# Low weight parts by accumulating DMA, the compression steps moved, and the last block of the last projection in halves

## The chip, the core and the metric

The kernel runs on one core of one Trainium2 chip. The core has TensorE (PE in the profile; its weight loads are shown as PEld), VectorE (DVE), ScalarE (ACT), GpSimd (POOL) and SyncE (SP), which issues the DMAs of this kernel. All engines run at the same time and wait for one another through semaphores. The metric is the device time of one execution in microseconds (us), as the median of several runs.

## What is computed

The reference is a small decoder trunk over 256 tokens of width 1024: one layer with a gated short convolution, one with a sparse attention, and around each mixer two half-step feed-forwards (d_ff = 2816). Between the two layers the keys and values are made once, among them a compressed set (blocks of 32 tokens through a small two-layer network). Cut to what the change touches:

```python
def swiglu_ffn(x, w_in, w_out):
    gate, up = jnp.split(x @ w_in, 2, axis=-1)
    return (jax.nn.silu(gate) * up) @ w_out

def compress(raw, pe, w1, w2):
    ...
    return jax.nn.gelu(blk @ w1) @ w2

def reference(x, ...):
    h = x
    for i in range(DEPTH):
        if i == N_A_LAYERS:
            kv = shared_kv(h, ...)
        h = h + 0.5 * swiglu_ffn(rmsnorm(h, ffn1_norm[i]), ffn1_w_in[i], ffn1_w_out[i])
        hn = rmsnorm(h, mix_norm[i])
        if i < N_A_LAYERS:
            h = h + short_conv_mixer(hn, conv_w_in[i], conv_w[i], conv_w_out[i])
        else:
            h = h + nsa_mixer(hn, attn_w_q[j], attn_q_norm[j], attn_w_o[j], rel_bias, kv)
        h = h + 0.5 * swiglu_ffn(rmsnorm(h, ffn2_norm[i]), ffn2_w_in[i], ffn2_w_out[i])
    return h
```

All inputs and the output are float32.

## The kernel before, in words

**Split products.** Every large product is made of three: each operand is split into a high part, rounded to the type fp32r, and a low part, the rest. The product is high x high, low x high and high x low. With the activations as the moving operand (512 columns: 256 tokens of the high part and 256 of the low part side by side) a weight tile of 128 x 128 takes two matmuls: its high part against all 512 columns and its low part against the 256 columns of the high part. Method half (L430) issues them; a_pass runs all high ones of a group and then all low ones, or the other way round, and each call begins with the kind with which the call before ended (turn).

**The weight stream.** Class Stream brings the weights in. A chunk of 2048 columns (1 MB) is loaded by SP into one of three staging buffers (tile ws, L197). A chunk holds two units of 1024 columns; a unit is 8 weight tiles. Method high casts a unit on ScalarE into a tile wh (L238). Method low subtracts on VectorE: wl = ws - wh (L266). Six buffers exist for each of wh and wl, used in turn, so a unit takes the buffers of the unit six places before, and its cast and its subtraction wait until PE has done with those. A staging buffer is free for the next load when both of its units have been read. Method pump emits high and low of the next units wherever PE's program has given buffers back (done). Units are numbered in the order of use: 0 to 43 are the first feed-forward's in projection (two a step, 22 steps), 44 to 65 its out projection, 66 to 89 the convolution's in projection (three a step).

**In and out projections.** ffn_in runs 22 steps f of two units (gate and up), 16 matmuls of each width; the evacuation of a step (ffn_evac, called through weave, which pumps the stream between its parts) runs on ScalarE and VectorE under the next step. out_proj makes 8 blocks c of the output; each takes 22 weight tiles in a row of the stream, that is 2.75 units. After each block out_evac adds it to h and prepares the next stage's operand: ScalarE and VectorE split it into xs, GpSimd sums its squares.

**Background of the second layer's first feed-forward.** Function bg(f) is called after step f of that ffn_in and holds what makes the shared keys and values: k_trans (transposes of the keys through PE), rh_split (split of the raw blocks), c_hidden (16 matmuls of 256 columns with the two units of a compression weight, W1AT tells after which step), c_total (its halves added by a small product, then gelu on GpSimd), c_second, kc_norm, kc_trans and c_values. The compression weights stand in the stream behind the units of step W1AT[0] and W1AT[1].

**The last out projection.** out_pairs makes the last projection into the output from 11 pairs p of inner blocks. For a pair not in PLAIN it uses seven products of sums in place of eight (a scheme in the manner of Strassen and Winograd); for a pair in PLAIN the eight plain ones. A product is three matmuls of 512 columns (L1415), here with the activations as the stationary operand. The sums of weights and of activations for the first kind are made on VectorE (sums, L167, and Pairs.add). Each pair's weights are prepared one or two pairs ahead (prepare, with pair_high, L161, and pair_low, L172). The eight products collect in eight banks m[1] to m[8]; m[1], m[6], m[7] and m[5] are shared by several output blocks, m[2], m[3], m[4] and m[8] belong to one each. After the last seven-product pair (last) the shared sums go through ScalarE, VectorE and GpSimd into p11, p12, p21 and p22, while PE does the remaining plain pairs; then each block gets its own bank added (L1432) and is stored (L1444).

Nothing plans this order at run time: each engine's program is as the code emits it, and each works it off in that order.

Of the kernel before, what the change touches and what calls it, by code (L numbers as in the profile page):

```python
# [9 lines left out]
F32 = mybir.dt.float32  # L10
# [3 lines left out]
ALU = mybir.AluOpType  # L14
# [48 lines left out]
def trunk(ctx, tc, A, out):  # L63
# [45 lines left out]
    class Stream:  # L109
# [133 lines left out]
        def low(self):  # L243

            if not self.half:
                return
            half = self.half.pop(0)
            if len(half) == 6 and not isinstance(half, list):
                self.pair_low(*half)
                return  # L250
            if isinstance(half, list):
                for v, t in half:
                    ve.tensor_tensor(out=t[:, :, 1], in0=v, in1=t[:, :, 0].bitcast(F32), op=ALU.subtract)
                self.units.append(tuple(t for _, t in half))
                return
            src, h = half
            if isinstance(h, Halves):
                l = Halves()
                for x in range(2):
                    ve.tensor_tensor(out=l.t[x], in0=src[:, x * 512:(x + 1) * 512], in1=h.t[x].bitcast(F32), op=ALU.subtract)  # L260
                self.units.append((h, l))
                return
            l = mk([P, 1024], "wl", NBUF, F32R)
            if len(src.shape) == 3:
                l = l.rearrange("p (a n) -> p a n", n=512)
            ve.tensor_tensor(out=l, in0=src, in1=h.bitcast(F32), op=ALU.subtract)  # L266
            if len(src.shape) == 3:
                h, l = [t.rearrange("p a n -> p (a n)") for t in (h, l)]
            self.units.append((h, l))
# [19 lines left out]
                self.pump()  # L289

    W = Stream()
    W1AT = (11, 14)
    W.add(A["ffn1_w_in"][0])
    W.add(A["ffn1_w_out"][0])
    W.add(A["conv_w_in"])
# [14 lines left out]
    W.spare = set(range(len(W.where) - 2, len(W.where) + 1))  # L310
    W.add(A["ffn2_w_in"][1])
    NP = NF // 2
    PLAIN = (0, 2, 4, 6, 8, 10)
    TURNS = (3, 5, 7, 9)

    def second_home(p):
# [675 lines left out]
    def bg(f):  # L992
# [7 lines left out]
                po.tensor_tensor(out=v, in0=v, in1=r[:, tt * 8:tt * 8 + 8, None].to_broadcast([P, 8, 64]), op=ALU.mult)  # L1000
        elif f in (2, 4, 5, 8):
            c_blocks((2, 4, 5, 8).index(f))
        elif f in (6, 7):
            k_trans(f - 6)
        elif f == 9:
            kv["rk"] = rh_split(0)
        elif f == 10:
            kv["rv"] = rh_split(1)
            W.limit = NBUF
        elif f == W1AT[0]:  # L1010
            kv["ak"] = c_hidden(kv["rk"])
        elif f == 12:
            kv["ak"] = c_total(kv["ak"])
        elif f == W1AT[1]:
            kv["av"] = c_hidden(kv["rv"])
        elif f == 15:
            kv["av"] = c_total(kv["av"])
            kv["kc"] = kc_norm(c_second(kv["ak"], 0))
        elif f == 17:
            kc_trans(kv["kc"])  # L1020
        elif f == 18:
            c_values(kv["av"])

    hid = ffn_in(xs, None, R1, bg)
# [369 lines left out]
    def out_pairs(left, rows):  # L1394
# [7 lines left out]
        for p in range(NP):  # L1402
# [2 lines left out]
                todo[p] = {n: [(x, b[i]), (y, b[i + 2])] for n, i, x, y in ((2, 0, a11, a12), (3, 1, a11, a12), (4, 0, a21, a22), (8, 1, a21, a22))}  # L1405
            else:
                todo[p] = {n: [(left[p][n - 1], right[n])] for n in right}
        total = {n: sum(len(t.get(n, ())) for t in todo.values()) for n in m}

        def product(p, *which):  # L1410
            for n in which:
# [32 lines left out]
            sy.dma_start(out[tt * P:(tt + 1) * P, 512 * x + c.start * P:512 * x + c.stop * P], o[:, c].rearrange("p a m -> p (a m)"))  # L1444

        W.freed += 1 << 10
        last = max(p for p in range(NP) if p not in PLAIN)
        for p in range(last + 1):
            product(p, *(2, 4 if p else 8) if p in PLAIN else (1, 2))
            prepare(p)  # L1450
# [8 lines left out]
        u3 = add(u2, 7, u2, None)  # L1459
        p21, p22 = plus(u3, 1, hT[1, 0]), plus(u3, 1, hT[1, 1])  # L1460
        for n, tt, x, o in ((2, 0, 0, p11), (3, 0, 1, p12), (4, 1, 0, p21), (8, 1, 1, p22)):
            for p in range(last + 1, NP):
                product(p, n)
            if n == 3:
                add(p12, 5, p12, 0)
                add(p22, 5, p22, 1)
            for c in (slice(0, 2), slice(2, 4)) if n == 8 else (slice(0, 4),):
                store(tt, x, add(o, n, o, tt, c), c)

    out_pairs(hid.left, X["rows"])  # L1470

# [69 lines left out]
```

## Time and profile before

| | |
|---|---|
| median of 3 runs | 967.3 us (966.65 to 968.2) |
| profiled execution, own time | 967.22 us |
| its span, first to last instruction | 965.4 us |
| granted TensorE clock | 0.999 |
| VectorE subtractions of the stream (L266, from ws) | 263, 326.2 us in all |
| ScalarE casts of the stream (L238, from ws) | 263, 272.2 us in all |
| read from HBM | 175.52 MB, 183 GB/s over the span |

How to read the lines: a line of a group names the code line, the engine, the operation, the tile written and those read, the shapes and the count; then the busy time, the mean duration of one in ns, and the idle time of the engine just before them with what ended most of it. A line in order of time begins with the start and the time in us, and ends with the idle time before it, where there was any, and the engine that ended it. A line of stretches gives the stretch, its length, then for PE, PEld, DVE, ACT and POOL the busy time and the number of instructions, the granted clock, the DMA engines' busy share and GB/s. Matmuls overlap: one of 512 columns is listed with 0.39 us, but the next can start before its end, so the distance of starts is what it costs.

The 40 slices of the page, each 24.1 us:

```profile
PE   9999999999999999999999999999999999999998
DVE  6988776668889888767659788866588788878896
ACT  7665553355556665644548787653579656656563
POOL 1000001144470100011321021001337350000002
DMA  7665554545536974555535556454520354467362
```

### The profile page before, as it was taken

The page shows a single profiled execution, that of the slowest core. Times are in us where ns is not written, and L with a number is a line of the kernel's source. Part 1 is how long each engine was busy: PE and PEld are TensorE (multiplying, and loading weights), DVE is VectorE, ACT ScalarE, POOL GpSimd, SP SyncE. Part 2 cuts the span into 40 slices and gives each one's busy share as a digit, 9 for nine tenths or more (in the row PEclk, how much of TensorE's full clock was granted, in tenths as well). Part 3 has the DMA queues.
Part 4 walks back from the last instruction along what each step waited for, and adds up shares of the span by engine and source line. Part 5 has one row for each costly group of instructions (what it writes and reads, how often), then busy time and mean ns, then how long its engine had stood idle before and what let it go on. Part 6 is the DMA issues. An engine that isn't in the chain of part 4 may idle for free.

```text
span 965.4 us, 14668 instructions
## 1 busy us (share of the span) xinstructions
PE 958.4 (99%) x5597; PEld 839.1 (87%) x5597; DVE 754.2 (78%) x1212; ACT 582.0 (60%) x982; POOL 173.0 (18%) x266
## 2 busy tenths in 40 slices
PE   9999999999999999999999999999999999999998
PEld 7888888888888888888888888888987888888886
DVE  6988776668889888767659788866588788878896
ACT  7665553355556665644548787653579656656563
POOL 1000001144470100011321021001337350000002
PEclk9999999999999999999999999999999999999999
DMA  7665554545536974555535556454520354467362
GB/s 294 231 213 180 187 206 175 186 166 210 188 135 228 272 238 176 188 204 182 211 131 182 192 206 251 174 189 168 218 89 1 132 218 155 152 217 257 106 205 88
DMA packets 36422, 178.60 MB, mean 185 GB/s; under 512 B 3424, under 2 KB 7152, under 8 KB 18560
## 3 DMA queue, kind: packets, MB, share of 16 engines
q1 hardware_dynamic: 36352, 177.67, 52.1%
q8 instruction: 44, 0.72, 0.3%
q14 instruction: 26, 0.21, 0.1%
HBM read 175.52 MB, written 1.08 MB: 183 GB/s over the span
## 4 chain that ended last, share of the span: by engine, by line
PE 94%; DVE 2%; ACT 2%; DMA 1%; issue 0%; SPq 0%; DVEq 0%
PE mm L430 53%; PE a L430 26%; PE a L1415 4%; PE mm L1415 2%; PE mm L1181 1%; PE a L1246 1%; PE a L812 1%; PE a L814 1%; PE a L813 1%; DMA base<-in_first_dram 1%; PE a L1226 1%; PE mm L655 1%; PE a L694 1%; DVE pr L1189 0%; ACT act L914 0%; ACT pr L1200 0%
## 5 line engine op out<-in xcount | busy, mean ns | idle before, releaser
L266 DVE TENSOR_TENSOR wl<-ws,wh 128x1024 fp32r<-128x1024 f32 x263 | 326.2, 1251 | 67.6 <-ACT wh L238 41.6
L430 PE MATMUL mm<-xs,wh 128*128 128x512 f32 x1480 | 348.8, 390 | 0.0
L430 PEld LDWEIGHTS mm<-xs,wh 128*128 128x128 f32 x1480 | 273.7, 188 | 54.3 <-DVE xs L383 0.2
L238 ACT CAST wh<-ws 128x1024 fp32r<-128x1024 f32 x263 | 272.2, 1046 | 35.6 <-PE a L430 21.1
L430 PEld LDWEIGHTS mm<-xs,wl 128*128 128x128 f32 x1480 | 185.5, 192 | 4.3
L430 PE MATMUL mm<-xs,wl 128*128 128x256 f32 x1480 | 188.3, 283 | 0.0
L430 PE MATMUL a<-act,wh 128*128 128x512 f32 x608 | 141.7, 390 | 0.0
L430 PEld LDWEIGHTS a<-act,wh 128*128 128x128 f32 x608 | 113.0, 188 | 22.7
L449 DVE TENSOR_TENSOR t<-mm,t 128x512 f32<-128x512 f32 x95 | 65.2, 686 | 61.1 <-ACT t L448 60.5
L448 ACT COPY t<-mm 128x512 f32<-128x512 f32 x95 | 55.5, 584 | 75.5 <-PE mm L430 75.1
L430 PEld LDWEIGHTS a<-act,wl 128*128 128x128 f32 x608 | 75.7, 192 | 1.6
L430 PE MATMUL a<-act,wl 128*128 128x256 f32 x608 | 76.4, 283 | 0.0
L473 ACT ACTIVATE t<-t 128x256 f32<-128x256 f32 x88 | 36.8, 419 | 56.5 <-DVE t L460 56.4
L379 ACT ACTIVATE xs<-base 128x256 fp32r<-128x256 f32 x48 | 24.1, 506 | 77.5 <-DVE base L573 62.1
L460 DVE TENSOR_TENSOR t<-t,R 128x512 f32<-128x512 f32 (+1 forms) x88 | 57.1, 649 | 2.6
L442 ACT CAST act<-t 128x256 fp32r<-128x256 f32 x91 | 37.0, 407 | 28.8 <-DVE t L743 18.2
L397 POOL TENSOR_TENSOR t<-base 128x256 f32<-128x256 f32 x35 | 26.2, 750 | 134.7 <-DVE base L573 108.5
L394 POOL TENSOR_TENSOR sq<-base 128x256 f32<-128x256 f32 x5 | 3.1, 613 | 229.2 <-DVE base L573 220.8
L443 DVE TENSOR_TENSOR act<-t,act 128x256 fp32r<-128x256 f32 x91 | 39.0, 428 | 5.7 <-ACT act L442 5.7
L383 DVE SCALAR_TENSOR_TENSOR xs<-base,xs 128x256 fp32r<-128x256 f32 x48 | 29.4, 616 | 17.5 <-ACT xs L379 17.4
L474 DVE TENSOR_TENSOR t<-t,t 128x256 f32<-128x256 f32 x88 | 36.9, 419 | 4.0 <-ACT t L473 3.9
L1440 POOL TENSOR_TENSOR t<-t,base 128x512 f32<-128x512 f32 x4 | 5.1, 1292 | 166.9 <-ACT t L1438 166.9
(313 smaller groups left out, 1144.9 us busy)
## 6 DMA issues: line engine op xcount, KB each, us to landing
ws<-in_ffn_w_in_dram SPq DMA_DIRECT2D x69, 1024.0 KB, 4.8
ws<-in_ffn_w_out_dram SPq DMA_DIRECT2D x33, 1024.0 KB, 4.6
ws<-in_conv_w_in_dram SPq DMA_DIRECT2D x12, 1024.0 KB, 4.6
base<-in_ffn_w_in_dram SPq DMA_DIRECT2D x11, 1024.0 KB, 5.2
ws<-in_w_kv_dram SPq DMA_DIRECT2D x6, 1024.0 KB, 4.8
base<-in_ffn_w_pairs_dram SPq DMA_DIRECT2D x12, 512.0 KB, 4.9
kt<-in_ffn_w_in_dram SPq DMA_DIRECT2D x5, 1024.0 KB, 7.6
ws<-in_conv_w_out_dram SPq DMA_DIRECT2D x4, 1024.0 KB, 4.8
```

Of the source, the lines that this page charges most:

```text
L238: ac.copy(h, src)
L266: ve.tensor_tensor(out=l, in0=src, in1=h.bitcast(F32), op=ALU.subtract)
L383: ve.scalar_tensor_tensor(out=xs[c][:, T:], in0=h[c], scalar=gt[:, g + c:g + c + 1], in1=xs[c][:, :T].bitcast(F32), op0=ALU.mult, op1=ALU. ...
L430: pe.matmul(o if x == 0 else o[:, :T], u[x][:, q * P:(q + 1) * P], rhs if x == 0 else rhs[:, :T], start=start, stop=stop, skip_group_check ...
L442: ac.copy(dst[:, :T], src)
L443: ve.tensor_tensor(out=dst[:, T:], in0=src, in1=dst[:, :T].bitcast(F32), op=ALU.subtract)
L448: ac.copy(r, o[:, :, T:])
L449: ve.tensor_tensor(out=r, in0=o[:, :, :T], in1=r, op=ALU.add)
L460: ve.tensor_tensor(out=r, in0=r, in1=R[:, None, :].to_broadcast([P, n, T]), op=ALU.mult)
L473: ac.activation(s, r[:, 0], AF.Silu)
L474: ve.tensor_tensor(out=s, in0=s, in1=r[:, 1], op=ALU.mult)
L1415: pe.matmul(m[n], x, w, start=(count[n] == 0 and i == 0), stop=(count[n] == total[n] - 1 and i == 2), skip_group_check=True)
```

## The change

Three edits.

1. In Stream.low, the units whose number is in BYDMA = range(12, 80, 4) don't get their low part from VectorE. ScalarE writes -src into the low tile, whose type rounds it as the cast rounds the high part; then GpSimd issues a DMA that adds src to it.
2. In bg, k_trans of both halves and both c_hidden are called after step 13 (before: 6, 7, 11 and 14), both c_total after 15 (12 and 15), c_second and kc_norm after 17 (15), kc_trans and c_values after 19 (17 and 18). W1AT = (13, 13) puts both compression weights behind step 13 in the stream.
3. PLAIN has pair 9 in place of pair 8, so that the last seven-product pair is 8 and two plain pairs, 9 and 10, come after it. The last block (p22) gets its m[8] of the earlier pairs added ahead of time; its products of pairs 9 and 10 are made in two halves of 256 columns, each in a bank of its own, and each half is added and stored by itself.

```diff
@@ Stream.low
             l = mk([P, 1024], "wl", NBUF, F32R)
             if len(src.shape) == 3:
                 l = l.rearrange("p (a n) -> p a n", n=512)
-            ve.tensor_tensor(out=l, in0=src, in1=h.bitcast(F32), op=ALU.subtract)
+            if len(self.units) in BYDMA:
+                ac.activation(l, src, AF.Copy, scale=-1.0)
+                po.dma_start(l, src, accum_op=ALU.add)
+            else:
+                ve.tensor_tensor(out=l, in0=src, in1=h.bitcast(F32), op=ALU.subtract)
@@ trunk
-    W1AT = (11, 14)
+    W1AT = (13, 13)
...
-    PLAIN = (0, 2, 4, 6, 8, 10)
+    BYDMA = range(12, 80, 4)
+    PLAIN = (0, 2, 4, 6, 9, 10)
@@ bg
-        elif f in (6, 7):
-            k_trans(f - 6)
...
         elif f == W1AT[0]:
-            kv["ak"] = c_hidden(kv["rk"])
-        elif f == 12:
-            kv["ak"] = c_total(kv["ak"])
-        elif f == W1AT[1]:
-            kv["av"] = c_hidden(kv["rv"])
+            for tt in range(2):
+                k_trans(tt)
+            kv["ak"], kv["av"] = c_hidden(kv["rk"]), c_hidden(kv["rv"])
         elif f == 15:
-            kv["av"] = c_total(kv["av"])
+            kv["ak"], kv["av"] = c_total(kv["ak"]), c_total(kv["av"])
+        elif f == 17:
             kv["kc"] = kc_norm(c_second(kv["ak"], 0))
-        elif f == 17:
+        elif f == 19:
             kc_trans(kv["kc"])
-        elif f == 18:
             c_values(kv["av"])
@@ out_pairs
-        total = {n: sum(len(t.get(n, ())) for t in todo.values()) for n in m}
+        last = max(p for p in range(NP) if p not in PLAIN)
+        total = {n: sum(len(t.get(n, ())) for p, t in todo.items() if n != 8 or p <= last) for n in m}
...
         for n, tt, x, o in ((2, 0, 0, p11), (3, 0, 1, p12), (4, 1, 0, p21), (8, 1, 1, p22)):
+            if n == 8:
+                for c in (slice(0, 2), slice(2, 4)):
+                    z = bank([P, 2, P])
+                    left = [(xs, [t[:, at, c.start * P:c.stop * P] for t in W.pair[p, kind]]) for p in range(last + 1, NP) for xs, (kind, at) in todo[p][8]]
+                    for k, ((xh, xl), (wh, wl)) in enumerate(left):
+                        for i, (a, w) in enumerate(((xh, wh), (xl, wh), (xh, wl))):
+                            pe.matmul(z.rearrange("p a m -> p (a m)"), a, w, start=(k == 0 and i == 0), stop=(k == len(left) - 1 and i == 2))
+                    ve.scalar_tensor_tensor(out=p22[:, c], in0=z, scalar=rows[:, 1:2], in1=p22[:, c], op0=ALU.mult, op1=ALU.add)
+                    store(1, 1, p22, c)
+                break
             for p in range(last + 1, NP):
                 product(p, n)
-            if n == 3:
+            if n == 2:
                 add(p12, 5, p12, 0)
+            store(tt, x, add(o, n, o, tt))
+            if n == 2:
                 add(p22, 5, p22, 1)
-            for c in (slice(0, 2), slice(2, 4)) if n == 8 else (slice(0, 4),):
-                store(tt, x, add(o, n, o, tt, c), c)
+                add(p22, 8, p22, 1)
```

More of the change, by code (lines that the diff above doesn't have):

```diff
@@ L1446, in out_pairs @@
         W.freed += 1 << 10
-        last = max(p for p in range(NP) if p not in PLAIN)
         for p in range(last + 1):
```

## The prediction

> **What bounds the kernel now.** I read the page first (busy shares, then the chain that ended last), then the busy time by stretches, the waits of TensorE's weight loads between 24 and 473 us, and the instructions in order of time at the places that the change touches.
>
> ```profile
> span 965.4 us, 14668 instructions
> PE 958.4 (99%) x5597; PEld 839.1 (87%) x5597; DVE 754.2 (78%) x1212; ACT 582.0 (60%) x982; POOL 173.0 (18%) x266
> PE 94%; DVE 2%; ACT 2%; DMA 1%; issue 0%; SPq 0%; DVEq 0%
> L266 DVE TENSOR_TENSOR wl<-ws,wh 128x1024 fp32r<-128x1024 f32 x263 | 326.2, 1251 | 67.6 <-ACT wh L238 41.6
> 22.00:473.00 451.00, 451.00 (x2592) 398.98 (x2591) 353.98 (x472) 252.47 (x367) 83.09 (x107) 1.00 0.57 199
> PEld mm L430 <- DVE xs L383: 0.2, 1, 0.2
> 24.98 105.59 PE mm L430 x608
> 130.57 61.09 PE a L430 x352
> ```
>
> TensorE is busy for 99% of the span. A busy PE need not be at its peak, so the second question is whether its matmuls follow one another at a fixed pace. They do:
>
> ```profile
> 67.36 4.00 PE L430 MATMUL mm<-xs,wl 128*128 128x256 f32 x32
> 71.19 7.44 PE L430 MATMUL mm<-xs,wh 128*128 128x512 f32 x32
> 78.47 1.72 PE L430 MATMUL mm<-xs,wl 128*128 128x256 f32 x13
> ```
>
> From 67.36 to 71.19 are 32 matmuls of 256 columns, 0.120 us each; from 71.19 to 78.47 are 32 of 512 columns, 0.2275 each. The chain holds the same pace: 608 matmuls, half of each width, in 105.59 us are 0.1737 each, the mean of the two. In the 451 us from 22 to 473 PE shows no idle time and its loads waited 0.2 us. So in the stage where VectorE is relieved, nothing waits for VectorE, and every microsecond for which PE is made to wait is added to the end. Gains can come only from places where PE waits or the tail runs alone.
>
> **The change part by part.**
>
> *First feed-forward, low parts.* Units 12, 16, ... 76 (17 of them, range(12, 80, 4)) lose a VectorE subtraction of 1.22 us each. That is some 21 us of VectorE, worth nothing by the rows above. Added on each: one ScalarE copy (the cast of the same size takes 1.04), a GpSimd DMA that reads the staged unit and adds it into the low tile (512 KB), and PE's wait for its landing. The question is which units have their low part ready soon enough. In the steady part of the feed-forward:
>
> ```profile
> 64.41 1.05 ACT L238 CAST wh<-ws 128x1024 fp32r<-128x1024 f32 x1
> 65.88 1.22 DVE L266 TENSOR_TENSOR wl<-ws,wh 128x1024 fp32r<-128x1024 f32 x1
> ```
>
> This is unit 24; its low matmuls are those at 78.47 in the fence above. Low part ready at 67.10: 11.4 us of lead. With the copy at 65.5 to 66.5, a transfer may take 11.9 us before PE waits. The staging buffer is held until landing, so the load that reuses it starts some 4 us later; the casts are also about 10 us ahead of PE, which hides it. ScalarE's extra 17 us over some 190 us (it is busy 252 of 451 us) hides in its idle time.
>
> The out projection is different. Each output block uses 22 weight tiles, a unit has 8, and blocks alternate in the order of their high and low passes, so two low passes stand back to back. Unit 52 is the ninth of the projection: tiles 64 to 71, of which block 2 (tiles 44 to 65) needs two at the end of its low pass.
>
> ```profile
> 137.80 5.40 PE L430 MATMUL a<-act,wh 128*128 128x512 f32 x23
> 143.04 5.44 PE L430 MATMUL a<-act,wl 128*128 128x256 f32 x44
> 148.31 10.16 PE L430 MATMUL a<-act,wh 128*128 128x512 f32 x44
> 140.36 3.07 ACT L238 CAST wh<-ws 128x1024 fp32r<-128x1024 f32 x3
> 143.53 3.50 DVE L266 TENSOR_TENSOR wl<-ws,wh 128x1024 fp32r<-128x1024 f32 x3 [2.56 <-PE a L430]
> 139.99 0.61 POOL L394 TENSOR_TENSOR sq<-base 128x256 f32<-128x256 f32 x1 [120.10 <-DVE base L573]
> 148.06 0.61 POOL L397 TENSOR_TENSOR t<-base 128x256 f32<-128x256 f32 x1 [7.45 <-DVE base L573]
> ```
>
> The 44 low matmuls at 143.04 are blocks 1 and 2. The first two finish unit 46, whose low buffer (six of them in turn) unit 52 takes: hence VectorE's 2.56 us wait until 143.53. The 43rd, at 143.04 + 42 x 0.120 = 148.07, is the first use of unit 52. Today 143.53 + 1.22 leaves 3.3 us. In the changed kernel ScalarE waits in VectorE's place, ends its copy at about 143.53 + 1.05 = 144.6, and the transfer has 148.07 - 144.6 = 3.5 us. Behind the waiting copy on ScalarE stand the casts of units 53 and 54, not needed before 153; on GpSimd nothing stands before 148.06, so the DMA goes out at once.
>
> No row of this trace shows an accumulating DMA or one issued by GpSimd. The nearest:
>
> ```profile
> base<-t SPq DMA_DIRECT2D x16, 64.0 KB, 2.1
> out_dram<-t SPq DMA_DIRECT2D x3, 256.0 KB, 2.0
> ws<-in_ffn_w_out_dram SPq DMA_DIRECT2D x33, 1024.0 KB, 4.6
> base<-in_ffn_w_pairs_dram SPq DMA_DIRECT2D x12, 512.0 KB, 4.9
> kt<-in_ffn_w_in_dram SPq DMA_DIRECT2D x5, 1024.0 KB, 7.6
> ```
>
> Lower end 2.0 us (half the bytes, a plain store), upper end 7.6 (the slowest issue of 1024 KB). An add has to read both operands, so 512 KB of result are 1024 KB read: the row of 4.6 is the nearest, and with 0.2 for the step from ScalarE to GpSimd I take 4.8. Then unit 52 is there at 149.4, and PE waits 1.3 us (0 at the lower end, 4.1 at the upper).
>
> The Trainium skill weighs in here: "Collectives: The Full Stack", section The bandwidth ceiling: the fold count and why AG ≠ RS ≠ AR, says that the add in the DMA path costs no time itself but two source reads. "DMA: Bandwidth & Descriptors", section Anatomy of one DMA — SWDGE (gpsimd) path, gives 2.0 us plus bytes over 436 GB/s; with 1.05 MB read that is an estimate of 4.4 us, and the sum below would be 0.4 lower. The row of 4.6 agrees within 0.2; an add by DMA no run here shows yet.
>
> The second narrow place is unit 72, in the conv projection:
>
> ```profile
> 200.67 1.05 ACT L238 CAST wh<-ws 128x1024 fp32r<-128x1024 f32 x1
> 201.97 1.31 DVE L266 TENSOR_TENSOR wl<-ws,wh 128x1024 fp32r<-128x1024 f32 x1
> 201.59 0.61 POOL L754 TENSOR_TENSOR R<-R 128x256 f32<-128x256 f32 x1 [4.77 <-DVE R L412]
> 208.43 2.08 PE L430 MATMUL mm<-xs,wl 128*128 128x256 f32 x16
> ```
>
> The copy would end at 202.8, and PE starts this low pass at 208.43: 5.6 us. At 4.8 it costs nothing, at 7.6 it costs 2.0. GpSimd's conv products (L729 to L735) queue behind the DMA; they feed only the out projection much later. The nearest of the others is unit 56, eight tiles into block 4:
>
> ```profile
> 151.31 1.05 ACT L238 CAST wh<-ws 128x1024 fp32r<-128x1024 f32 x1 [0.75 <-PE a L430]
> 158.31 1.96 PE L430 MATMUL a<-act,wl 128*128 128x256 f32 x15
> ```
>
> Its copy would end at 153.4; blocks 3 and 4 run their low passes from 158.31, and its first tile is the 31st matmul, at 161.9: 8.5 us, enough at either end.
>
> *Compression moved* (k_trans, both hidden products at f = 13, both totals at 15, the rest at 17 and 19). PE's products are the same ones.
>
> ```profile
> 573.36 0.52 PEld L936 LDWEIGHTS a<-both,t 128*128 128x128 f32 x4 [0.26 <-ACT t L928]
> 601.14 3.81 PE L430 MATMUL mm<-xs,wh 128*128 128x512 f32 x16
> 605.11 3.92 PE L430 MATMUL mm<-xs,wh 128*128 128x512 f32 x16
> ```
>
> At f = 12 the total's product waits 0.26 us for ScalarE's copy, made one step earlier; two steps later it will not. After the small products the next 16 matmuls take 3.92 instead of 3.81; such returns fall from six (f = 6, 7, 12, 15, 17, 18) to four. I take -0.26 - 2 x 0.1 = about -0.4, bounds -0.7 and +0.5 (the four hidden-layer units are now eaten in a row, 3.9 us of PE for 5 us of VectorE, covered by the pair of matmul groups on either side).
>
> *Last projection.* Pair 8 takes the seven-product form and pair 9 the plain one: as many products as before. Pairs 7 and 8 are now neighbours, and VectorE's sums and splits bunch:
>
> ```profile
> 938.12 2.36 DVE L172 TENSOR_TENSOR wl<-kt,wh 128x1024 fp32r<-128x1024 f32 x2 [0.47 <-ACT wh L161]
> 940.40 3.49 DVE L172 TENSOR_TENSOR wl<-base,wh 128x1024 fp32r<-128x1024 f32 x3
> 944.41 2.67 DVE L167 TENSOR_TENSOR base<-base 128x1024 f32<-128x1024 f32 x3
> 944.78 0.62 PE L1415 MATMUL a<-wh,act 128*128 128x512 f32 x2
> ```
>
> Two low parts of pair 8 (1.2 + 0.7) slip in ahead of 938.12, so pair 7's end at 941.2; sums (2.67) to 943.9; casts and low parts of pair 8's other kinds to 946.3 and 947.4. PE starts pair 8 at 945.46 (944.78 plus three matmuls) and after two products, 6 x 0.227 = 1.36, wants the first at 946.8: a lead of 0.5 to 1 us. No wait; if a cast slips by 2 us, +1.
>
> The end:
>
> ```profile
> 960.95 0.39 PE L1415 MATMUL mm<-wl,act 128*128 128x512 f32 x1
> 961.38 0.88 DVE L1432 SCALAR_TENSOR_TENSOR t<-mm,sm,t 128x256 f32<-128x256 f32 x2 [0.47 <-PE mm L1415]
> ```
>
> Today both half evacuations (0.44 each) follow the last matmul. In the changed kernel the first half's runs under the second half's twelve matmuls (1.44 us), so one goes: -0.44. For it PE does 24 matmuls of 256 columns instead of 12 of 512: 24 x 0.120 - 12 x 0.227 = +0.16. Net -0.3 (bounds -0.7, the whole pair and its store; +0.4, if VectorE's added sums delay the first half). With 48 closing matmuls instead of 24, the sums of the four blocks have more cover than now.
>
> Sum: 0 for VectorE, +1.3 unit 52, 0 unit 72, -0.4 compression, -0.3 tail = +0.6. The profiled execution took 967.2 (span 965.4 and 1.8 around it), the median of the runs shown is 967.3: the forecast is 967.9.
>
> **Rivals.**
>
> 1. *The transfer is slow: PE waits instead of VectorE* (slower). At 7.6 us unit 52 costs 4.1, unit 72 2.0; less 0.7 that is +5.4: 972.7. For it: the 7.6 row, DMA engines 57% busy in this stretch. Against: unit 52's transfer meets few loads, since their staging buffers are just being freed. It decides from about 6.0 us per transfer, where the sum passes +1.9.
> 2. *The transfer is quick, 3.5 us or less*: no wait at all, only compression and tail remain, -0.7: 966.6. For it: 2.0 and 2.1 us for smaller copies. Against: twice the bytes of the largest of these.
> 3. *VectorE does slow PE in a way that no wait shows* (faster). If a tenth of the 21 us came back, 964.5. Against it: the even pace of 0.120 and 0.2275.
> 4. *The change doesn't do what it says*: the tail saves nothing because the first half's evacuation stands behind the other blocks' on VectorE; +0.4 instead of -0.3, so 968.6. It lies inside the forecast's own range.
>
> **How the numbers follow.** Forecast with rival 4 (transfer of 3.8 to 6 us): 0.42. Rival 2: 0.25. Rival 1: 0.26. Rival 3: 0.07. About 0.2% (1.9 us) is what a measurement of this kernel can tell from no change. Faster by more: 0.07 (rival 3). Within: the forecast and rival 2, 0.67. Slower: 0.26. The range leaves out most of rival 3 and the part of rival 1 beyond its worked price: 966.2 (rival 2 with the tail's better bound) to 972.7.
>
> **What would show it.** A PE wait for a DMA near 148 and none near 78: unit 52. Low tiles landing within 3.5 us of their copy: rival 2; over 6: rival 1, with a second wait near 208. No wait of c_total's load for L928. One evacuation of 256 columns, not two, behind the last matmul. PE pace below 0.2275: rival 3. Wrong would be: a wait elsewhere in the first feed-forward (transfers near 12 us), or PE idle between 945 and 950.

## The result, and the profile after

The changed kernel took 974.4 us (median of 4 runs, 973.99 to 974.54) against 967.26 us of the kernel before on the same chip. The ratio is 1.0075, with a 95% interval of 1.0063 to 1.0087: some 7.1 us slower. The forecast was 967.9 with a range up to 972.7, so the time lies beyond the range, in the direction of rival 1.

From the page of the changed kernel, the lines that answer to those of before. In the line of L270 (the subtraction, L266 before) the mean is in ns and stands behind the busy time; in the last line 8.6 is the median time in us from issue to landing.

```profile
span 972.2 us, 14733 instructions
...
PE 959.7 (99%) x5609; PEld 840.5 (86%) x5609; DVE 737.5 (76%) x1196; ACT 597.0 (61%) x999; POOL 187.5 (19%) x283
...
PEclk9999998999999999999999999999999999999999
...
L270 DVE TENSOR_TENSOR wl<-ws,wh 128x1024 fp32r<-128x1024 f32 x246 | 306.1, 1254 | 87.8 <-ACT wh L238 63.1
...
wl<-ws POOLq DMA_DIRECT2D x17, 512.0 KB, 8.6
```

The relief is there: 17 subtractions and 20 us of VectorE are gone. Two lines speak of the loss. The transfers take 8.6 us, not 4.8, and the seventh slice, from 146 to 170 us, has a lower TensorE clock. The instructions of TensorE in order of time show what happened there (start, duration, and in brackets the idle time before it):

```profile
142.88 5.19 PE L435 MATMUL a<-act,wl 128*128 128x256 f32 x42
154.17 0.80 PE L435 MATMUL a<-act,wl 128*128 128x256 f32 x2 [6.09 <-DMA wl<-ws]
154.76 11.55 PE L435 MATMUL a<-act,wh 128*128 128x512 f32 x44
166.15 5.44 PE L435 MATMUL a<-act,wl 128*128 128x256 f32 x44
171.42 1.78 PE L435 MATMUL a<-act,wh 128*128 128x512 f32 x7
```

These are the rows that the prediction showed of before at 143.04, 148.31 and 158.31: the low pass of blocks 1 and 2, then the high and low pass of blocks 3 and 4. After 42 matmuls, at the 43rd, TensorE stands still until unit 52's low part lands. It is the only wait of TensorE for a transfer in the whole trace. From the start of one low pass to the start of the next were 158.31 - 143.04 = 15.27 us; now they are 166.15 - 142.88 = 23.27. So 8.0 us are lost between these two rows, and they have two parts. The first matmul after the wait starts 154.17 - 142.88 = 11.29 us into the stretch; before, the 43rd started 42 x 0.120 = 5.04 us into it: 6.25 us of waiting. From there to the next low pass are 166.15 - 154.17 = 11.98 us; before, 15.27 - 5.04 = 10.23: another 1.75 us, while TensorE is busy all the time. The stretches of the changed kernel show why (stretch, its length, then busy time and number of instructions for PE, PEld, DVE, ACT and POOL, the granted clock, DMA share, GB/s):

```profile
154.00:156.00 2.00, 1.83 (x5) 1.59 (x6) 0.00 (x0) 0.00 (x0) 0.00 (x0) 0.50 0.43 82
156.00:158.00 2.00, 2.00 (x7) 1.55 (x6) 0.16 (x1) 1.04 (x1) 0.00 (x0) 0.58 0.96 393
```

The granted clock was 0.50 when the matmuls began again and stayed there until almost 158.

Where did the other edits end up? The compression lies between blocks 5 and 6 of this projection and the query projection. First the kernel before, then the changed one, each with the first matmul behind that stage; the start of the stretch is 163.59 in the first and 171.42 (last row of the low and high passes above) in the second.

```profile
163.59 9.71 PE L430 MATMUL a<-act,wh 128*128 128x512 f32 x42
689.12 0.28 PE L1102 MATMUL mm<-wh,xs 128*128 128x256 f32 x1
```

```profile
696.48 0.28 PE L1103 MATMUL mm<-wh,xs 128*128 128x256 f32 x1
```

689.12 - 163.59 = 525.53 us became 696.48 - 171.42 = 525.06: the moved compression gains 0.47 us. The wait for the copy of c_total is not among the waits any more.

The end of the changed kernel, in order of time:

```profile
967.54 0.48 DVE L1470 SCALAR_TENSOR_TENSOR t<-a,sm,t 128x256 f32<-128x256 f32 x1 [0.68 <-PE a L1469]
968.66 0.28 PE L1469 MATMUL a<-wl,act 128*128 128x256 f32 x1
968.98 0.48 DVE L1470 SCALAR_TENSOR_TENSOR t<-a,sm,t 128x256 f32<-128x256 f32 x1 [0.95 <-PE a L1469]
962.48 7.34 SPq L1446 DMA_DIRECT2D out_dram<-t  x5
```

The first half is evacuated at 967.54, under the second half's matmuls; one evacuation follows the last matmul. The last line spans SP's five issues of stores; its end, 969.82, is when the last store has been issued, 0.88 us after the last matmul's end (968.94). The kernel before:

```profile
958.16 4.58 SPq L1444 DMA_DIRECT2D out_dram<-t  x5
```

There the last store was issued at 962.74, 1.40 us after the last matmul's end at 961.34. So 0.52 us are saved behind the last matmul, and the 24 matmuls of half width cost 24 x 0.120 - 12 x 0.227 = 0.16: net -0.36. The traces give the same without that reckoning: from the first matmul of the last projection (at 904.25 us before and 911.70 now) to the last store's issue are 58.49 us before and 58.12 now. From the last store's issue to the end of the span the two differ too, 2.7 us before and 2.4 after; the experiments show that this belongs to no edit.

Sum by the rows: +8.0 (unit 52), -0.47 (compression), -0.36 (tail) = +7.2, against a difference of the medians of 7.1.

### The profile page after: what moved, and what is told of

The parts are those of the page before. It is cut to its first block, busy times and chain, and to the rows that moved or that the text cites. A ratio compares the mean times of both kernels' runs of the same rounds, so it can differ in the third digit from the quotient of the medians.

```text
span 972.2 us, 14733 instructions
## 1 busy us (share of the span) xinstructions
PE 959.7 (99%) x5609; PEld 840.5 (86%) x5609; DVE 737.5 (76%) x1196; ACT 597.0 (61%) x999; POOL 187.5 (19%) x283
## 4 chain that ended last, share of the span: by engine, by line
PE 95%; DMA 2%; DVE 1%; ACT 1%; issue 0%; SPq 0%
PE mm L435 54%; PE a L435 25%; PE a L1417 4%; PE mm L1417 2%; DMA wl<-ws 1%; PE mm L1182 1%; PE a L1247 1%; PE a L817 1%; PE a L818 1%; PE a L819 1%; PE a L1227 1%; DMA base<-in_first_dram 1%; PE mm L660 1%; PE a L699 1%; DVE pr L1190 0%; PE a L930 0%
## 5 line engine op out<-in xcount | busy, mean ns | idle before, releaser
L270 DVE TENSOR_TENSOR wl<-ws,wh 128x1024 fp32r<-128x1024 f32 x246 | 306.1, 1254 | 87.8 <-ACT wh L238 63.1
L435 PE MATMUL a<-act,wh 128*128 128x512 f32 x608 | 143.1, 392 | 0.0
L454 DVE TENSOR_TENSOR t<-mm,t 128x512 f32<-128x512 f32 x95 | 65.2, 686 | 56.4 <-ACT t L453 55.6
L268 POOL DMA_DIRECT2D wl<-ws x17 | 15.1, 889 | 128.6 <-ACT t L478 98.0
```

The source lines that it names most:

```text
L435: pe.matmul(o if x == 0 else o[:, :T], u[x][:, q * P:(q + 1) * P], rhs if x == 0 else rhs[:, :T], start=start, stop=stop, skip_group_check ...
L454: ve.tensor_tensor(out=r, in0=o[:, :, :T], in1=r, op=ALU.add)
```

## The experiments

**The theory.** Unit 52 alone makes the loss. A staging buffer is given back when a transfer lands, and SP then lets go two waiting loads of 1 MB. So the landing of unit 48's transfer sends 2 MB ahead of unit 52's. The wait that follows is long enough to bring the clock down. That the loads wait for the transfers is in the trace of the changed kernel, in SP's own waits from 30 to 150 us (us in total, times, longest):

```profile
SPq L197 <- DMA wl<-ws: 111.9, 11, 11.1
```

In the kernel before SP's loads wait for VectorE in the same stretch, and for no DMA. Two loads go at a time because SP works its loads off in order: when unit 48's transfer landed, at 143.0, the buffer of the second load had been read by VectorE since 140.8, and both loads were issued between 143.1 and 143.6.

**The rivals:** a lone transfer of this kind takes 8 to 9 us by itself; the loss is spread over the 17 transfers; the half pace comes from the traffic, not from the idle time.

### no_dma: no unit by DMA, the other two edits kept

```diff
-    BYDMA = range(12, 80, 4)
+    BYDMA = ()
```

> The changed kernel with no unit by DMA (compression moved, last block in halves). Theory (the one wait for unit 52 and the half clock after it are all of the loss; the lags read from the two traces are -0.45 us for the compression and -0.68 for the tail): 1.1 us under the kernel before, about 966.1. Rival (the rest of the loss lies in the moved steps): above 968.

Measured: 965.71 us, ratio 0.9987 (0.9979 to 0.9996). The DMAs are the whole loss, and the other two edits are a small gain: -1.3 us by the medians, of which the rows of its trace show -0.48 (compression) and -0.36 (tail). In its trace the remaining 0.5 lies ahead of both, where these edits change nothing: blocks 3 and 4 of the out projection end at 163.06 us, against 163.59 before and 163.71 in compress_only. Why is not shown.

### skip52: all units of the change but unit 52

```diff
-    BYDMA = range(12, 80, 4)
+    BYDMA = [u for u in range(12, 80, 4) if u != 52]
```

> 16 units by DMA, unit 52 by VectorE again. Theory: as no_dma within 0.4 us, no wait of PE for a DMA, no stretch below full clock; VectorE's 20 us of relief bring nothing. Rival 1 (relief helps where no wait shows): over 1 us below no_dma. Rival 2 (another unit waits once this one doesn't): a wait near 162 or 208 and over 1 us above no_dma.

Measured: 966.06 us, ratio 0.9992 (0.9983 to 1.0001); TensorE waits for no transfer. Sixteen of the seventeen transfers together cost 0.35 us against no_dma by the medians and gain nothing: the relief of VectorE was worth nothing, as the forecast had it. Eight of the eleven executions lie at 965.4 to 966.1 us, as those of no_dma do; three lie at 967.0 to 967.5. The profiled one is of the eight, so what cost the three some 1.4 us is not shown. The loss of 8 us hangs on one unit.

### only52: unit 52 alone

```diff
-    BYDMA = range(12, 80, 4)
+    BYDMA = (52,)
```

> Unit 52 alone by DMA. Theory (its transfer stood behind two 1 MB loads that the landing of unit 48's transfer had let go): no load in flight, first packet about 1.5 us after the issue, landing 4.4 us after the issue, PE waits 1.3 us instead of 6.1, no fall of the clock; 1.4 above no_dma. Rival (an accumulating DMA issued by GpSimd takes 8 to 9 us by itself): PE waits about 6 us, half clock follows, 7 to 8 us above no_dma.

Measured: 967.51 us, ratio 1.0006 (0.9996 to 1.0015). The same low pass in this run:

```profile
143.10 5.19 PE L435 MATMUL a<-act,wl 128*128 128x256 f32 x42
149.67 0.51 PE L435 MATMUL a<-act,wl 128*128 128x256 f32 x2 [1.38 <-DMA wl<-ws]
...
160.02 5.44 PE L435 MATMUL a<-act,wl 128*128 128x256 f32 x44
```

The wait is 1.4 us and no half pace follows: 160.02 - 149.67 = 10.35 us to the next low pass. By itself the edit costs what the forecast had put down for it. What differs is what the DMA engines did in the first 4.5 us after the issue. By the view of the DMA queues (packets, MB, share of 16 engines), from 144.8 to 149.3 us in the changed kernel:

```profile
q1 hardware_dynamic: 204, 1.54, 98.0%
```

and from 144.9 to 149.3 us in only52:

```profile
q0 software_dynamic: 144, 0.52, 62.3%
```

Queue q1 holds SP's loads, q0 the accumulating transfer. In the changed kernel not one packet of the transfer moved in that time: the loads had the engines to themselves. In only52 the whole transfer was done within it. The Trainium skill, "DMA: Bandwidth & Descriptors", section Issuing engines are not separate DMA queues, says that DMAs of several issuers share the 16 engines and interleave. The sharing is in these rows; the interleaving is not, as the 2 MB let go ahead of the transfer went nearly wholly before it. In another run (warm, below) the two queues did mix: 125 packets of the transfer and 73 of the loads between 145.3 and 149.3 us.

### two: units 48 and 52

```diff
+    BYDMA = (48, 52)
```

> Units 48 and 52 by DMA. Theory (48's held staging buffer and the loads behind it delay 52's transfer): landing of 52's later than alone by 1 to 4 us, PE waits 2.5 to 5 us. Rival (each transfer has its own time, whatever the loads): as only52.

Measured: 967.44 us, ratio 1.0005 (0.9996 to 1.0014), a wait of 1.3 us. The expectation of 2.5 to 5 us missed. The stretches just before and after unit 52's transfer was issued, at 145.1 us:

```profile
142.50:144.80 2.30, 2.30 (x18) 2.14 (x17) 0.00 (x0) 1.11 (x2) 0.00 (x0) 1.00 1.01 427
144.80:147.00 2.20, 2.20 (x21) 2.20 (x20) 1.28 (x2) 1.83 (x2) 0.91 (x1) 1.00 0.45 134
```

The two loads that unit 48 let go ran at 427 GB/s until about 145 and were out of the way. So the theory had to be changed. A transfer that meets no loads lands some 4.5 us after its issue; the two loads that it frees take some 6.4 us more (in this run issued at 138.7, done at 145.1), and from one such unit to the next are 11.1 us: a chain on time just stays on time. A chain that is once late, landing after 8 to 9 us, lets its loads go so late that they are still under way at the next issue, and each transfer makes the next one late. Two runs put this to the test.

### start28: the chain begins at unit 28 in place of 12

```diff
-    BYDMA = range(12, 80, 4)
+    BYDMA = range(28, 80, 4)
```

> Units 28, 32, ..., 76 go by accumulating DMA; units 12 to 24 keep VectorE's subtraction. Theory: the lateness is a state that feeds itself. A transfer that meets no loads lands about 4.2 us after it is issued; its landing then frees a staging buffer for two loads of 1 MB, which take about 6.3 us at the 330 GB/s of these stages, together 10.5 to 10.7 us, a little less than the 11.1 us from one such unit to the next: a chain that starts on time stays on time, and only one that has once been late (in the changed kernel at units 16 to 24) queues behind loads each time. If the state was begun by units 12 to 24, then unit 28 on land about 4.5 us after their issue, TensorE's wait at unit 52 is 1.3 to 2 us, no half clock follows, and the time is about 967.5. Rival: the queue grows along any long chain, however it starts (seven transfers up to unit 52): landings of 7 us and more again, a wait of 3 to 6 us at unit 52, 970 to 974.5 us. That two transfers in a row were not enough (run two) speaks for neither.

Measured: 967.5 us, ratio 1.0005 (0.9995 to 1.0014), a wait of 1.3 us at unit 52. Issue to landing (min/median/max) of the seven transfers of units 28 to 52:

```profile
DMA to landing us min/median/max: 4.5/4.5/4.8
```

and of units 24 to 52 in the changed kernel:

```profile
DMA to landing us min/median/max: 8.6/9.4/10.0
```

Seven transfers in a row, none late. The rival, a queue that grows along any chain, is out for these seven. The six behind unit 52 took 4.6 to 8.4 us, and TensorE waited for none of them.

### skip48: the full chain without unit 48

```diff
-    BYDMA = range(12, 80, 4)
+    BYDMA = [u for u in range(12, 80, 4) if u != 48]
```

> All 17 units but unit 48, which keeps VectorE's subtraction. Theory: unit 52's transfer comes late because the landing of unit 48's frees two loads of 1 MB 1.4 to 1.8 us ahead of it. Without unit 48's transfer those loads are let go earlier, unit 52's transfer meets an empty or nearly empty queue as in run only52 and lands about 4.4 us after its issue: a wait of 1.3 to 2 us at unit 52, no half clock, about 967.5 us. Rival: the delay is made by the whole run of transfers before (their sum of bytes, or the loads that they have put off), not by the one just before: a wait of 3 to 6 us and 970 to 974.5.

Measured: 967.45 us, ratio 1.0002 (0.9993 to 1.0012), a wait of 1.4 us. Issue to landing of the transfers of units 24 to 44 and, in the second fence, of unit 52:

```profile
DMA to landing us min/median/max: 9.3/9.6/9.9
```

```profile
DMA to landing us min/median/max: 4.6/4.6/4.6
```

The chain was in the late state up to unit 44; one link left out, and unit 52 is on time. The delay comes from the transfer just before, through the loads that it holds back.

### warm: TensorE kept busy in the place of the wait

```diff
+    W.fill, NFILL = True, 27
...
+                        if (c, x, k, W.fill) == (2, 1, 20, True):
+                            W.fill, z = False, bank()
+                            for i0 in range(NFILL):
+                                pe.matmul(z, ones.bitcast(F32R), lhs[0], start=True, stop=True)
```

> The changed kernel, with 27 matmuls of 512 columns put on TensorE where it waits for unit 52's low part (about 27 x 0.23 = 6.1 us at full pace); their result is not used. Theory: 1.7 us of the loss is TensorE's half pace after an idle stretch of 6.1 us. With the stretch filled the wait shrinks to under 1 us, no matmul after it runs at 0.427 us, the windows from 147 to 158 show a granted clock near 1.0, and the time is 1.0 to 2.0 us under the changed kernel's 974.4: about 972.7. Rival: the slow matmuls after the wait have another cause (their operands, the transfers still running): then they stay slow and the time is 974.4 or above.

Measured: 973.66 us, ratio 1.0068 (1.0054 to 1.0081). By the time it stays undecided: 0.7 us under the changed kernel, less than expected, and the intervals overlap. The trace:

```profile
143.38 5.19 PE L436 MATMUL a<-act,wl 128*128 128x256 f32 x42
148.41 6.48 PE L616 MATMUL a<-act,ones 128*128 128x512 f32 x27
154.73 0.40 PE L436 MATMUL a<-act,wl 128*128 128x256 f32 x2
...
164.97 5.43 PE L436 MATMUL a<-act,wl 128*128 128x256 f32 x44
```

No half pace: 164.97 - 154.73 = 10.24 us, as before the change, and the whole stretch is 164.97 - 143.38 = 21.59 us, 1.68 less than the changed kernel's 23.27. But this run does not separate causes cleanly. In the profiled execution unit 52's transfer landed 5.0 us after its issue, so the 27 matmuls were the whole delay, and the traffic differed from that of the changed kernel. The transfers of units 24 to 52 in it landed 5.0 to 7.5 us after their issue (median 6.0).

Up to unit 52 this program is that of the changed kernel, yet its chain recovered: the late state is not reached in every execution.

### late52_2 and late52_1: a lone transfer, issued late

Run only52 with one or two multiplications by ones on GpSimd ahead of the issue, so that TensorE waits longer without any chain of transfers.

```diff
                 ac.activation(l, src, AF.Copy, scale=-1.0)
+                for i0 in range(2):
+                    v = ...
+                    po.tensor_tensor(out=v, in0=v.bitcast(F32), in1=ones[:, None, :].to_broadcast([P, 8, P]), op=ALU.mult)
                 po.dma_start(l, src, accum_op=ALU.add)
```

> Run only52 (unit 52 alone by accumulating DMA), with two multiplications of the 128x1024 tile by ones on GpSimd between ScalarE's copy and the transfer's issue, each 2.3 to 3.5 us by the 0.60 and 0.88 us that GpSimd takes for 256 columns. The transfer meets no more loads than in only52; it starts later, so TensorE waits 1.4 + 4.6 to 7.0 = 6.0 to 8.4 us at unit 52. Theory (TensorE runs at half pace after an idle stretch of this length, whatever the DMA queues do): the first matmuls of 512 columns after the wait are 0.427 us apart for about 3 us, the granted clock there falls as in the changed kernel, and 1.5 to 1.8 us come on top of the wait: lag behind only52 = added wait + 1.7, time 973.7 to 976.2. Rival (the slow matmuls come from the transfers and loads that run beside them, or the operands): no half pace, lag = added wait alone, 972.1 to 974.5; the lag in the trace, not the time, tells them apart.

> The same with one multiplication in place of two: TensorE waits 1.4 + 2.3 to 3.5 = 3.7 to 4.9 us at unit 52. It places the idle length from which the half pace follows, between the 1.4 us that left the clock at 1.00 and the 6.1 us that halved it. If a stretch of about 4 us is enough: 0.427 us between the matmuls after it for 1 to 3 us, lag behind only52 = added wait + 0.5 to 1.7 us, time 970.3 to 972.7. If it is not: pace 0.2275 us throughout, lag = added wait, 969.8 to 971.0.

Measured with two: 975.73 us, ratio 1.0091 (1.0076 to 1.0107). With one: 972.22 us, ratio 1.0055 (1.0041 to 1.0068). In both the wait, the half pace and the time came out as the theory had them, but with two multiplications the half pace costs more. The low passes, and the stretches of 1 us in which the granted clock falls and comes back (for one multiplication with a row between them), first with two multiplications:

```profile
142.53 5.19 PE L438 MATMUL a<-act,wl 128*128 128x256 f32 x42
154.98 0.77 PE L438 MATMUL a<-act,wl 128*128 128x256 f32 x2 [7.26 <-DMA wl<-ws]
...
167.93 4.24 PE L438 MATMUL a<-act,wl 128*128 128x256 f32 x34
```

```profile
150.00:151.00 1.00, 0.00 (x0) 0.00 (x0) 1.00 (x2) 0.00 (x0) 0.88 (x1) 0.69 0.00 0
160.00:161.00 1.00, 1.00 (x5) 0.78 (x4) 0.00 (x0) 0.10 (x1) 0.00 (x0) 0.69 0.48 90
```

then with one:

```profile
142.85 5.19 PE L438 MATMUL a<-act,wl 128*128 128x256 f32 x42
152.02 0.48 PE L438 MATMUL a<-act,wl 128*128 128x256 f32 x2 [3.98 <-DMA wl<-ws]
...
163.94 5.43 PE L438 MATMUL a<-act,wl 128*128 128x256 f32 x44
```

```profile
152.00:153.00 1.00, 0.98 (x5) 0.89 (x6) 0.00 (x0) 0.00 (x0) 0.00 (x0) 0.87 0.44 66
154.00:156.00 2.00, 2.00 (x6) 1.52 (x6) 0.96 (x1) 1.01 (x1) 0.00 (x0) 0.50 0.95 389
156.00:157.00 1.00, 1.00 (x6) 0.80 (x5) 0.27 (x1) 0.09 (x1) 0.00 (x0) 0.92 0.14 57
```

and the same two stretches of the changed kernel:

```profile
150.00:151.00 1.00, 0.00 (x0) 0.00 (x0) 0.95 (x3) 0.00 (x0) 0.00 (x0) 0.93 0.97 274
157.00:158.00 1.00, 1.00 (x5) 0.78 (x4) 0.16 (x1) 0.80 (x1) 0.00 (x0) 0.66 0.97 410
```

From the first matmul after the wait to the next low pass: 12.95 us after a wait of 7.3, 11.92 after one of 4.0, 11.98 in the changed kernel after 6.1, 10.35 in only52 after 1.4. So an idle stretch brings the half pace without any late chain; the rival of traffic falls: between 154 and 156 us the clock is at 0.50 beside 389 GB/s with one multiplication, while in only52 it is at 1.00 beside 365 GB/s between 152 and 154. The price of the half pace, 2.6, 1.6 and 1.6 us over only52, does not follow the length of the wait. With two multiplications it is 0.9 more than expected.

The stretches show what it follows. On one side of each the clock reads 1.00 and on the other 0.50, so the value in between places the edge: 0.93 from 150 to 151 in the changed kernel means a fall at 150.86. By this estimate the clock was at half from 150.38 to 160.62 with two multiplications, from 152.74 to 156.16 with one, and from 150.86 to 157.68 in the changed kernel: 10.24, 3.42 and 6.82 us, that is three times, once and twice 3.4. Only the part in which TensorE had work costs anything: from the restart at 154.98, from the fall at 152.74 and from the restart at 154.17 these are 5.64, 3.42 and 3.51 us. Half of them, 2.8, 1.7 and 1.8, is the loss against the full pace, and 12.95, 11.92 and 11.98 less the 10.23 of the kernel before are 2.7, 1.7 and 1.75. By these three waits the price hangs on where the restart falls in the steps of 3.4 us, not on how long the wait was.

The Trainium skill, "TensorE: Matmul & The Clock Gate", section What's actually happening, has the clock halve after at least one idle window of about 3.4 us, in windows that run on freely. The steps of 3.4 us agree, and so do 1.4 us of idle time without and 4.0 with a halved clock. That the idle time must fill a whole window does not: in the changed kernel the clock fell 2.8 us after the last matmul's end at 148.07, with two multiplications 2.7 us after that at 147.72.

### compress_only: the kernel before with the moved compression alone

```diff
-    W1AT = (11, 14)
+    W1AT = (13, 13)
...
+            kv["ak"], kv["av"] = c_total(kv["ak"]), c_total(kv["av"])
```

> The kernel before, with the move of the compression's steps alone (start at feed-forward step 13 for both halves, totals at 15, normalisation at 17, the rest at 19). Theory: the two waits for the totals go and the moved steps hide: -0.35 to -0.55 us, the lag after that stage -0.45, about 966.8. Rival: within the whole change the gain hung on the transfers having emptied VectorE; alone the moved steps meet VectorE's low parts and cost 0 to +0.5 us, 967.2 to 967.8.

Measured: 966.26 us, ratio 0.9992 (0.9983 to 1.0000). In the trace the same stretch as above is 688.76 - 163.71 = 525.05 us, 0.48 less than before:

```profile
163.71 9.48 PE L430 MATMUL a<-act,wh 128*128 128x512 f32 x41
688.76 0.28 PE L1098 MATMUL mm<-wh,xs 128*128 128x256 f32 x1
```

Its end is that of before, instruction by instruction, yet from the last store's issue (957.84 + 4.58 = 962.42) to the end of the span (964.8) are 2.4 us, against 2.7 in the kernel before. So 0.3 us of scatter lie in the landing of the last store. The rows bear the theory out (0.45 forecast for this stage, 0.48 found), and the moved steps do not need the transfers. The time is 0.8 below that of before and its interval just reaches 1.0000.

### tail_only and halves_only: the end alone

tail_only is the kernel before with the halves and the new split of pairs; halves_only keeps the old split:

```diff
+    PLAIN = (0, 2, 4, 6, 8, 10)
```

> The kernel before, with the last product's halves and the new split of plain and paired steps alone; no accumulating DMA, the compression as before. Theory: the tail's gain stands by itself: +0.15 us up to the last matmul, -0.8 to -0.9 behind it (one evacuation of 0.44 and one store's issue of 0.4 less in the chain), -0.65 to -0.75 in all, about 966.5. Rival: part of it came with the compression's move: -0.3, about 966.9.

> The kernel before, with the last product's halves but the old split (step 8 plain, step 9 paired). After the last paired step fewer steps are then left for the last product: one plain step of six matmuls per half in place of two. Theory: what follows the last matmul is the same (-0.8 to -0.9), and the time is that of tail_only within 0.3 us, so that the new split is worth little by itself. Rival: with too few matmuls in the halves the evacuations of the products before are not covered and the last matmul comes 0.3 us or more later: no gain or half of it, 966.8 to 967.3.

Measured: tail_only 966.67 us, ratio 0.9997 (0.9989 to 1.0006); halves_only 967.57 us, ratio 1.0007 (0.9998 to 1.0015). By the time neither theory nor rival of tail_only is decided, as its interval holds both. By the trace the expected -0.7 had taken the store's landing for a part of the edit. Its last store is issued at 955.05 + 7.32 = 962.37, 0.37 before that of the kernel before, and its end comes 2.6 to 2.7 us later:

```profile
955.05 7.32 SPq L1450 DMA_DIRECT2D out_dram<-t  x5
```

The theory of halves_only missed. The last matmul and VectorE's last work in its trace:

```profile
960.67 0.28 PE L1473 MATMUL a<-wl,act 128*128 128x256 f32 x1
959.83 1.40 DVE L1438 SCALAR_TENSOR_TENSOR t<-a,sm,t 128x512 f32<-128x512 f32 x2
961.14 0.87 DVE L1474 SCALAR_TENSOR_TENSOR t<-a,sm,t 128x256 f32<-128x256 f32 x2
```

With one closing pair VectorE is still at the other blocks until 961.2, past the last matmul's end at 960.95. Both halves are evacuated behind it, and the edit has only its cost: from the first matmul of the last projection to the last store's issue are 58.49 us before, 58.13 in tail_only and 58.83 here. The rival had the cause (evacuations that are not covered) but not the place: the last matmul ends only 0.07 us later than before on this scale, and 0.27 are lost behind it. The times, 0.9 us apart, fit with it. The new split is what makes room for the halves.

## Why the prediction was wrong, and where it was right

**The step that failed** is the argument against rival 1: "unit 52's transfer meets few loads, since their staging buffers are just being freed". The freeing is the trouble. The prediction knew that a buffer is held until landing and that the load behind it "starts some 4 us later", but asked only whether the casts would wait for that load, and not which transfer the load would stand ahead of. The landing lets SP send 2 MB ahead of the transfer (rows of the two queues), and with the buffer held until landing the lateness hands itself on from unit to unit (start28 and skip48 against the changed kernel). The term of the sum that was mis-sized is unit 52's transfer: 4.8 us from the end of ScalarE's copy. In the changed kernel ScalarE's copy ended at 144.4; the transfer, issued at 144.8, landed 9.3 us later, 9.7 us in all. The upper end of 7.6 was no bound either: it was a load's duration in the trace of before, where no such transfer held a buffer. The term as forecast, 1.3 us, is what only52 shows (1.4), so the duration was right for a lone transfer, and for a chain on time (start28), and wrong for a chain that runs late. Rival 1 did not happen as it was written either: of its two waits only the one at unit 52 came.

**What was not in the sum at all** is the half pace after a long wait: 1.75 us. Rival 1 priced its own wait without it, and so its 972.7, the top of the range, was too low although the range reached as far as that rival's worked price. With 8.0 in place of 1.3 the forecast's sum is 967.2 + 8.0 - 0.4 - 0.3 = 974.5; measured were 974.4. One sum of the prediction is off in a side remark: with its estimate of 4.4 us for the transfer the forecast would be 0.2 lower, not 0.4, as the 0.2 for the step from ScalarE to GpSimd stays.

**Right** were these steps:

- VectorE's relief is worth nothing (skip52 is not below no_dma), and rival 3 with it.
- The place: the 43rd low matmul of blocks 1 and 2, and no other wait in the feed-forward, although the transfers took up to 10.0 us there, within the 11.9 us of room. Unit 56 did not wait either.
- Unit 72: no wait. Its transfer met no loads and landed 4.6 us after the issue, within the 5.6 us of room.
- The compression: -0.4 forecast, -0.47 and -0.48 measured, and the wait for c_total's copy (0.26) is gone. That the rest comes from fewer returns to the large matmuls, as forecast, no row here shows.
- The tail: -0.3 forecast, -0.36 and -0.37 measured up to the last store's issue; one evacuation behind the last matmul, and no wait of TensorE between 945 and 950 us of the old time. Rival 4 did not happen in the changed kernel; halves_only shows it happening with the old split, at +0.34 where +0.4 was put on it.

**Where the lateness begins** can be read from the traces. A transfer and its two loads need about 10.9 us. In the changed kernel unit 20's transfer was issued 8.5 us after unit 16's (56.4 and 47.9 us), and it is the first to land clearly late, 7.7 us after its issue, with 161 packets of the loads and 37 of its own in the first 3.5 us. In warm and skip48 the gap is 8.4 and 8.5 us and the landing 7.1 and 8.2. start28 begins behind this place and its first seven are on time. So the short gap looks like the start of the lateness; no run took it away with the rest unchanged.

**Open** is why the chain stays late from there in some executions and recovers in others: from unit 24 on it took 8.6 to 10.0 us in the profiled execution of the changed kernel and 9.3 to 9.9 in that of skip48, but 7.5, falling to 5.0, in that of warm. The four times of the changed kernel, within 0.6 us of one another, fit with a late chain in each. A fourth staging buffer was not tried. Of the versions run, no_dma, with the compression and tail edits and without the DMAs, has the lowest median, below both kernels.

## What to carry to other kernels

When a copy is handed to the DMA queues, ask which buffer it holds until it lands, which loads wait for that buffer, and whether they will stand ahead of the next copy; a duration from a quiet queue says nothing about that chain. Where TensorE is the bound and a wait of several us is in sight (1.4 us did no harm here, 4.0 did, and nothing between was run), add the half pace behind it to the price: 1.6 to 2.6 us here. And take work off an engine only where a row shows somebody waiting for it: 20 us less on VectorE moved nothing here.

## What was not expected of the hardware

- **The clock.** An idle stretch of 4.0 us was followed by matmuls at a granted clock of 0.50; one of 1.4 us was not. In the run with 4.0 us the clock fell only 0.7 us after the matmuls had begun again (at 152.74 against 152.02). In the two longer waits it fell while TensorE stood idle, 2.7 and 2.8 us after the last matmul. It then stayed at half for once, twice or three times 3.4 us, so a wait of 6.1 us cost no more beyond itself than one of 4.0.
- **An accumulating DMA of 512 KB** from a tile into another takes 4.5 to 4.7 us from issue to landing alone, and up to 10.0 us behind two loads of 1 MB.
- **VectorE beside GpSimd.** With GpSimd multiplying a whole tile, VectorE's subtraction of 1.22 us took 2.61 and 3.36 us. These are the two subtractions of late52_2 between 145.0 and 150.9 us.
